# Opening of a two-layer trunk kernel: the modulation of chunks 6 and 7 computed by VectorE, and three scalings moved to ScalarE

## The chip, the cores and the metric

The kernel runs on one core of a Trainium2 chip. The metric is the device time of one execution in microseconds, the median of several runs. The engines of the core are TensorE (PE in the profile; its weight loads are PEld), VectorE (DVE), ScalarE (ACT) and GpSimd (POOL); SyncE (SP) issues most of the transfers from memory. Each engine works through a queue of its own in order, and engines wait for each other through semaphores.

## What is computed

The reference is a trunk of two layers over 512 tokens of width 1024 (a gated short convolution, then a state-space mixer, each followed by a SwiGLU network). Only its first steps matter here:

```python
mod = (jax.nn.silu(c) @ ada_w + ada_b).reshape(bsz, DEPTH, 2, 3, D_MODEL)
...
shift, scale, gate = (mod[:, i, 0, k][:, None, :] for k in range(3))
h = rmsnorm(x, norm_g[i, 0]) * (1.0 + scale) + shift
...
b_gate, c_gate, v = jnp.split(h @ w_in, 3, axis=-1)
u = causal_depthwise_conv(c_gate * v, conv_w)
return (b_gate * u) @ w_out
```

So a vector c of 1024 values is multiplied with columns of a wide matrix `ada_w` to give shift and scale, h is scaled and shifted with them, and h is multiplied with `w_in`. All of it is float32. A float32 product of the large kind is made of three products of rounded parts (high x high, high x low, low x high).

## The kernel before: how the opening is built

Channels lie in partitions: the 1024 channels are eight chunks (j = 0 to 7) of 128 partitions, and h_j is a tile of 128 x 512 (tokens) with a high and a low part. The opening builds h_0 to h_7 one by one, and uses each at once: six blocks of columns of `w_in` (128 columns each: two of c_gate, two of v, two of b_gate) are accumulated in six PSUM banks over the eight chunks, so that TensorE has work as soon as h_0 exists.

The order of all engines' instructions in this part is written out by hand in the table `OPENING`. Each name is a step, and each engine's queue holds its instructions in the order of the table. The names that matter:

- A*j*, E*j*, T*j*, R*j* (`ada_first`): shift and scale of chunk j. A: TensorE multiplies c with the 2 x 128 columns of `ada_w` for this chunk (16 products whose moving operand is the matrix; four strips of the array at once). E: ScalarE copies the result to `ada_acc`. T: TensorE transposes it, two products. R: VectorE sums the four strips, adds the bias, and makes the factor `acol`.
- u*j*, H*j*, l*j* (`make_h`): u is scale and shift by VectorE, H the same by ScalarE with rounding (the high part), l the difference of the two by VectorE (the low part).
- wcl*k*, wsl*k*, wcb*k*, wsb*k*: the weights of chunks k and k + 1 (from k = 2 on), rounded by ScalarE (c) and their low parts by VectorE (s); l is for column blocks 0 to 3, b for 4 and 5.
- k*j*_*i*: three matmuls of 512 columns, chunk j into column block i (high x high; high weight x low h; low weight x high h). k*j*_4 and k*j*_5 use the b weights.

The columns of `ada_w` come by SP's queue in the order of the code: `stage_cols(3, 2)` loads chunks 3 and 4 together, 256 columns (1 KB of each row), and at wsb1 `stage_cols(5, 2)` does so for 5 and 6, in four transfers of 512 KB. At A4 the weights of chunks 6 and 7 (three transfers) and `stage_cols(7, 1)` follow, which reads 128 columns (512 B of each row) in two transfers of 512 KB. At k2_5 ScalarE issues two small loads of its own, `rows` (the convolution's taps) and `dtb`.

Each transfer takes one of eight semaphores (DMAHW0 to DMAHW7) in turn; before it is issued it waits until the transfer before it on this semaphore has landed. The turns are given out in the order in which the compiler places the transfers, with those of SP and ScalarE mixed.

Behind the opening stands the loop of line 1047 and following over the remaining columns of `w_in`. Its first instructions on ScalarE are the copy c_sb of column block 0 (`gate_c(0)`), the rounding of the first weights (`split(0)`), and c_sb of block 1; on VectorE the low part of those weights (also `split(0)`) and cv = block 2 x c_sb (`gate_v(0)`). TensorE's first matmul of this loop (tile ip) uses the PSUM bank of block 2, which cv frees.

Of the kernel before, what the change touches and what calls it, by code (L numbers as in the profile page):

```python
# [8 lines left out]
F32 = mybir.dt.float32  # L9
# [7 lines left out]
P = 128  # L17
# [21 lines left out]
def trunk_kernel(  # L39
# [84 lines left out]
    def ada_madd(acc, w, k):  # L124
        if k == 0:
            dve.tensor_scalar(acc, w, csil[:, 0:1], None, MUL)
        else:
            dve.scalar_tensor_tensor(acc, w, csil[:, k:k + 1], acc, MUL, ADD)  # L128
# [223 lines left out]
    def make_h(s, j, hj, src, sl):  # L352

        n = sl.stop - sl.start
        q = s * 24 + j
        us = []

        def value():
            us.append(t2("u")[:, :n])
            dve.tensor_scalar(us[0], src, acol[:, s * 8 + j:s * 8 + j + 1], mods[:, q:q + 1], MUL, ADD)  # L360

        return (value, lambda: act.activation(hj[:, 0, sl], src, AF.Identity, bias=mods[:, q:q + 1],
                                       scale=acol[:, s * 8 + j:s * 8 + j + 1]),
                lambda: dve.tensor_tensor(hj[:, 1, sl], us[0], hj[:, 0, sl].bitcast(F32), SUB))
# [5 lines left out]
xo0 xo1 xo2 xo3 A0b xo4 E0 xo6 xo5 T0 wcl0 R0 u0 q7 H0 wsl0 wcb0 k0a0 l0 xo7 k0a1 k0a2 k0a3 wsb0  # L370
k0c0 k0_4 A1 k0_5 E1 wcl1 T1 k0c1 wcb1 R1 k0c2 k0c3 k0b0 u1 k0b1 H1 k0b2 wsl1 k0b3 l1 A2 wsb1 k1_0
E2 T2 k1_1 R2 wcl2 k1_2 u2 H2 k1_3 wsl2 k1_4 wcb2 l2 k1_5 wsb2 k2_0 k2_1 k2_2 A3 A4 E3 T3 E4 k2_3 R3
T4 u3 H3 k2_4 R4 k2_5 wcl4 l3 u4 H4 k3_0 wsl4 k3_1 wcb4 k3_2 l4 k3_3 wsb4 k3_4 k3_5 k4_0 A5 A6 E5 T5
E6 k4_1 R5 wcl6 T6 u5 k4_2 H5 R6 k4_3 u6 H6 k4_4 l5 wcb6 A7 l6 wsl6 k4_5 E7 T7 wsb6 k5_0 R7 k5_1 u7
k5_2 H7 k5_3 l7 k5_4 k5_5 k6_0 k6_1 k6_2 k6_3 k6_4 k6_5 k7_0 k7_1 k7_2 k7_3 k7_4 k7_5
"""


# [412 lines left out]
    with ExitStack() as ph:  # L791
# [79 lines left out]
        def stage_cols(j0, n):  # L871
            cols = ada_stage(j0, n, lambda: actp.tile([P, 8 // n, n * P], F32, tag="a", name="ada_st0"))
            staged.extend([(q, cols) for q in range(n)])

        xf = [xf2s[j // 2][:, j % 2, :] for j in range(KD)]
        xtr = []

# [24 lines left out]
        with tc.manual_schedule(engines={PE_ENGINE, mybir.EngineType.SP, mybir.EngineType.Activation,  # L902
# [68 lines left out]
            def kmm(kk, i, parts):  # L971
                k = kk % 2
                w, c0 = (lead[kk // 2][0], i * P) if i < 4 else (lead[kk // 2][1], (i - 4) * P)
                for part in parts:
                    pe.matmul(acc_of(i), w[:, part // 2, k, c0:c0 + P], h[kk][:, part % 2, :],  # L975
                              start=(kk, part) == (0, 0), stop=(kk, part) == (KD - 1, 2))

            def step(name):
                kind, i = name[:1], name[1:]
                if name[:2] == "xo":  # L980
                    turned_out(int(name[2:]))
                elif name == "q7":
                    xtr.append(aux_ps("xtr"))
                    for t in range(4):
                        turn(t, 7)
                    busy(acc_of(2)[:, :P], 5)
                    h.extend([hp.tile([P, 2, T], F32R, tag=f"h{j}", name=f"h{j}") for j in range(4, KD)])
                elif kind == "A":
                    j = int(i[0])
                    if j:  # L990
                        mods_[j] = ada_first(j, *staged[j], cpad)
                    next(mods_[j])
                    if j == 0:
                        busy(acc_of(2)[:, :P], 2)
                    if j == 4:
                        list(lead_load(3))
                        stage_cols(7, 1)
                elif kind in "ETR":
                    next(mods_[int(i)])
                elif kind in "uHl":  # L1000
                    j = int(i)
                    if j not in hdo:
                        hdo[j] = make_h(0, j, h[j], xf[j], FULL)
                    hdo[j]["uHl".index(kind)]()
                elif kind == "w":
                    kk = int(name[3:])
                    if kk // 2 not in lead:
                        lead_tiles(kk // 2)
                    lead_split(kk // 2, slice(kk % 2, kk % 2 + 1) if kk < 2 else slice(0, 2),
                               "lb".index(name[2]), "cs".index(name[1]))  # L1010
                    if name == "wsb1":
                        list(lead_load(2))
                        stage_cols(5, 2)
                elif name[:2] == "k0" and name[2] in "abc":
                    kmm(0, int(name[3]), ("abc".index(name[2]),))
                else:
                    kk, i = (int(q) for q in i.split("_"))
                    kmm(kk, i, (0, 1, 2))
                    if (kk, i) == (2, 5):
                        dma_s(rows[:24, 3, :], a_conv_w.rearrange("i k (r p) -> (i k r) p", p=P))  # L1020
                        dma_s(dtb[:NH], m_dt_bias.rearrange("i (r p) -> (i r) p", p=1))
                    if (kk, i) == (4, 5):
                        turned(rows[:24, 3, :], acw, 24)
# [1898 lines left out]
```

## Time and profile before

| | us |
|---|---|
| median of 3 runs | 1309.39 |
| lowest, highest run | 1309.07, 1309.95 |
| profiled execution, span from first to last instruction | 1307.2 |
| TensorE busy in the span | 1295.7 |
| opening: first ip matmul | 60.64 |

The profile has no other time of the profiled execution than its span. It is 2.2 us below the runs' median: starting and ending the program lie outside the span.

Rows of the timeline read: start in us, length in us, engine, line, operation, output<-inputs, shapes, and how many records the row merges; behind it, in brackets, how long the engine idled before and what ended that. A float32 product that isn't split into parts appears as two records. Rows of a table by stretches read: the stretch, its length, busy time of each engine with its records in brackets, the granted clock of TensorE, the share of the transfer engines and GB/s. Rows of groups end with busy us, mean ns of one, and idle time before.

### The profile page before, as it was taken

The numbers are of one execution on the slowest core, as the hardware profiler recorded it, in microseconds if no ns is written. First come the engines' busy times: TensorE is split into PE (matmuls) and PEld (weight loads), VectorE is DVE, ScalarE is ACT, GpSimd is POOL, SyncE is SP. The second block draws the span as 40 slices with busy tenths as digits, with TensorE's granted clock in tenths as the row PEclk, the third lists the DMA queues.
The fourth block names the chain that finished last, engine by engine and source line by source line (L and its number), as shares of the span: only waits on it lengthen the run. The fifth ranks groups of instructions, "written<-read, shape, count | busy, mean of one in ns | idle before, by whom it ended". The sixth has DMA issues, their size and how long they took to land.

```text
span 1307.2 us, 20568 instructions
## 1 busy us (share of the span) xinstructions
PE 1295.7 (99%) x7841; PEld 1140.6 (87%) x7841; DVE 1045.4 (80%) x1598; ACT 736.0 (56%) x1302; POOL 127.5 (10%) x156
## 2 busy tenths in 40 slices
PE   8999999999999999999999999999999999999998
PEld 7788889999988888898888888888899999998886
DVE  5587998978866986769899998987877777767888
ACT  5423466455532565656765567755764555544665
POOL 0000011111100230000000000000100121101320
PEclk9999999999999999999999999999999999999999
DMA  9779661799868984437664456614432788878961
GB/s 310 229 257 297 185 193 50 204 239 240 202 190 264 261 158 119 144 118 231 219 216 160 141 177 217 185 50 161 145 98 72 190 221 204 205 194 286 176 123 64
DMA packets 225942, 241.69 MB, mean 185 GB/s; under 512 B 10532, under 2 KB 177588, under 8 KB 224820
## 3 DMA queue, kind: packets, MB, share of 16 engines
q1 hardware_dynamic: 203200, 192.87, 47.3%
q0 software_dynamic: 18496, 35.92, 15.1%
q10 hardware_dynamic: 4148, 11.59, 2.7%
q8 instruction: 61, 1.00, 0.3%
q14 instruction: 37, 0.30, 0.1%
HBM read 203.76 MB, written 4.34 MB: 159 GB/s over the span
## 4 chain that ended last, share of the span: by engine, by line
PE 94%; DMA 2%; SPq 2%; DVE 1%; ACT 1%; issue 0%; DVEq 0%
PE sA L693 12%; PE ip L305 11%; PE ip L307 11%; PE ip L306 11%; PE y L408 7%; PE sC L693 6%; PE cA L2624 5%; PE sB L693 3%; PE cA L1483 3%; PE li L305 2%; PE li L307 2%; PE li L306 2%; PE li L975 2%; PE y L1156 1%; PE y L2199 1%; PE yd L2027 1%
## 5 line engine op out<-in xcount | busy, mean ns | idle before, releaser
L305 PE MATMUL ip<-h,whl 128*128 128x512 f32 x640 | 253.0, 395 | 0.2 <-DVE cv L1075 0.2
L307 PE MATMUL ip<-h,whl 128*128 128x512 f32 x640 | 249.7, 390 | 0.0
L306 PE MATMUL ip<-h,whl 128*128 128x512 f32 x640 | 249.6, 390 | 0.0
L305 PEld LDWEIGHTS ip<-h,whl 128*128 128x128 f32 x640 | 120.3, 188 | 25.8 <-issue 1.8
L307 PEld LDWEIGHTS ip<-h,whl 128*128 128x128 f32 x640 | 120.3, 188 | 25.3
L306 PEld LDWEIGHTS ip<-h,whl 128*128 128x128 f32 x640 | 120.4, 188 | 23.8
L693 PE MATMUL sA<-tq,whl 128*128 128x256 f32 x1008 | 130.6, 284 | 0.0
L693 PEld LDWEIGHTS sA<-tq,whl 128*128 128x128 f32 x1008 | 125.5, 192 | 0.3
L232 DVE TENSOR_TENSOR whl<-wst,whl 128x1024 fp32r<-128x1024 f32 x70 | 85.2, 1220 | 23.4 <-ACT whl L231 22.3
L128 DVE SCALAR_TENSOR_TENSOR ada_acc<-ada_st,csil,ada_acc 128x1024 f32<-128x1024 f32 x70 | 89.7, 1282 | 3.2 <-DMA ada_st<-in_ada_w_dram 1.9
L305 PE MATMUL li<-h,whl 128*128 128x256 f32 x288 | 83.7, 290 | 0.0
L307 PE MATMUL li<-h,whl 128*128 128x256 f32 x288 | 81.7, 284 | 0.0
L306 PE MATMUL li<-h,whl 128*128 128x256 f32 x288 | 81.6, 283 | 0.0
L231 ACT CAST whl<-wst 128x1024 fp32r<-128x1024 f32 x70 | 72.6, 1040 | 7.8 <-DMA wst<-in_a_w_in_dram 4.0
L408 PE MATMUL y<-whlo,ys 128*128 128x512 f32 x288 | 67.3, 392 | 0.0
L1870 DVE SCALAR_TENSOR_TENSOR cu<-ip,cols,cu 128x511 f32<-128x511 f32 (+2 forms) x84 | 62.8, 747 | 3.4 <-ACT cu L1867 1.4
L408 PEld LDWEIGHTS y<-whlo,ys 128*128 128x128 f32 x288 | 53.8, 188 | 11.4 <-issue 0.5
L2624 PE MATMUL cA<-whlo,ao 128*128 128x512 f32 x264 | 61.0, 391 | 0.4 <-DVE c L2830 0.2
L2624 PEld LDWEIGHTS cA<-whlo,ao 128*128 128x128 f32 x264 | 49.4, 188 | 11.5 <-ACT whlo L2589 1.2
L305 PEld LDWEIGHTS li<-h,whl 128*128 128x128 f32 x288 | 55.3, 192 | 0.8 <-issue 0.8
L306 PEld LDWEIGHTS li<-h,whl 128*128 128x128 f32 x288 | 55.3, 192 | 0.0
L307 PEld LDWEIGHTS li<-h,whl 128*128 128x128 f32 x288 | 55.2, 192 | 0.0
(457 smaller groups left out, 2740.8 us busy)
## 6 DMA issues: line engine op xcount, KB each, us to landing
ada_st<-in_ada_w_dram SPq DMA_DIRECT2D x96, 512.0 KB, 6.4
wsu<-in_f_w_in_dram SPq DMA_DIRECT2D x30, 512.0 KB, 5.5
sg<-in_f_w_in_dram SPq DMA_DIRECT2D x56, 256.0 KB, 3.4
wsu<-in_f_w_in_dram SPq DMA_DIRECT2D x56, 256.0 KB, 4.7
wst<-in_m_w_in_dram SPq DMA_DIRECT2D x14, 1024.0 KB, 5.9
wst<-in_f_w_in_dram SPq DMA_DIRECT2D x10, 1024.0 KB, 5.1
wst<-in_m_w_in_dram SPq DMA_DIRECT2D x20, 512.0 KB, 5.2
wst<-in_a_w_in_dram SPq DMA_DIRECT2D x9, 1024.0 KB, 6.8
```

The costliest lines, as they stand in the source:

```text
L128: dve.scalar_tensor_tensor(acc, w, csil[:, k:k + 1], acc, MUL, ADD)
L231: later.append((lambda sw=sw, w=w: act.copy(w[:, 0, :nk, :], sw), lambda sw=sw, w=w: dve.tensor_tensor(w[:, 1, :nk, :], sw, w[:, 0, :nk, : ...
L232: lambda sw=sw, w=w: dve.tensor_tensor(w[:, 1, :nk, :], sw, w[:, 0, :nk, :].bitcast(F32), SUB)))
L305: pe.matmul(dst, w_at(w, 0, kk), a[:, 0, sl], start=start, stop=False)
L306: pe.matmul(dst, w_at(w, 0, kk), a[:, 1, sl], start=False, stop=False)
L307: pe.matmul(dst, w_at(w, 1, kk), a[:, 0, sl], start=False, stop=stop)
L408: pe.matmul(pst, a[:, al, tk], wt[:, wl, kk, :], start=i == 0 and k == (opens[hf][t] if opens else 0), stop=k == K - 1 and i == 2, skip_gr ...
L693: pe.matmul(dst, w[:, wl, k0 + k, :], self.moving(q, k, al), skip_group_check=True, start=q in self.FIRST and k == 0 and i == 0, stop=k == ...
L975: pe.matmul(acc_of(i), w[:, part // 2, k, c0:c0 + P], h[kk][:, part % 2, :], start=(kk, part) == (0, 0), stop=(kk, part) == (KD - 1, 2))
L1483: pe.matmul(bank[r, sub], a[:, al, q, tk], w[:, wl, q, :], start=first and k == 0, stop=False, skip_group_check=True)
L1870: dve.scalar_tensor_tensor(u[:, sft:], pst[:, :T - sft], w[3 - sft], u[:, sft:], MUL, ADD)
L2624: pe.matmul(bank[r][sub], a[:, al, q, tk], w[:, hl, q, :], start=first and k == 0, stop=last and k == 2, skip_group_check=True)
```

## The change

Chunks 6 and 7 no longer use `ada_first`. Their columns of `ada_w` are loaded by the new `stage_one`, shift and scale columns side by side, in four transfers of 256 KB for each chunk. Chunk 5 is loaded alone. VectorE multiplies with c's values and adds up, row block by row block (steps M*j*_0 to M*j*_7, `one_madd`, 128 x 256 each); TensorE sums over the partitions by two products with a column of ones (P*j*, `one_sums`); VectorE adds the bias and makes the factor (G*j*, `one_mods`). For chunks 5, 6 and 7 u is made by ScalarE. The last chunk's matmuls are put in another order: first and third part of all six blocks (k7d0 to k7d5), then the second parts (k7b0 to k7b5).

```diff
         def value():
             us.append(t2("u")[:, :n])
-            dve.tensor_scalar(us[0], src, acol[:, s * 8 + j:s * 8 + j + 1], mods[:, q:q + 1], MUL, ADD)
+            if j < 5:
+                dve.tensor_scalar(us[0], src, acol[:, s * 8 + j:s * 8 + j + 1], mods[:, q:q + 1], MUL, ADD)
+            else:
+                act.activation(us[0], src, AF.Identity, bias=mods[:, q:q + 1], scale=acol[:, s * 8 + j:s * 8 + j + 1])
...
-T4 u3 H3 k2_4 R4 k2_5 wcl4 l3 u4 H4 k3_0 wsl4 k3_1 wcb4 k3_2 l4 k3_3 wsb4 k3_4 k3_5 k4_0 A5 A6 E5 T5
-E6 k4_1 R5 wcl6 T6 u5 k4_2 H5 R6 k4_3 u6 H6 k4_4 l5 wcb6 A7 l6 wsl6 k4_5 E7 T7 wsb6 k5_0 R7 k5_1 u7
-k5_2 H7 k5_3 l7 k5_4 k5_5 k6_0 k6_1 k6_2 k6_3 k6_4 k6_5 k7_0 k7_1 k7_2 k7_3 k7_4 k7_5
+T4 u3 H3 k2_4 R4 k2_5 wcl4 l3 u4 H4 k3_0 wsl4 k3_1 wcb4 k3_2 l4 k3_3 wsb4 k3_4 k3_5 M6_0 M6_1 M6_2 M6_3
+k4_0 A5 E5 T5 k4_1 R5 u5 H5 M6_4 M6_5 M6_6 M6_7 k4_2 l5 k4_3 wcl6 k4_4 P6 G6 u6 H6 wsl6 wcb6 l6 k4_5 wsb6
+M7_0 M7_1 M7_2 M7_3 M7_4 M7_5 M7_6 M7_7 k5_0 k5_1 k5_2 k5_3 k5_4 k5_5 k6_0 k6_1 k6_2 P7 G7 H7 u7 l7 k6_3
+k6_4 k6_5 k7d0 k7d1 k7d2 k7d3 k7d4 k7d5 k7b0 k7b1 k7b2 k7b3 k7b4 k7b5
...
+        def stage_one(j):
+            one_st[j] = [actp.tile([P, 4, 2, P], F32, tag="a", name="ada_st1") for _ in range(2)]
+            for q, st in enumerate(one_st[j]):
+                for b in range(2):
+                    dma(st[:, :, b, :], ada_w[q * T:(q + 1) * T, b * D + j * P:b * D + (j + 1) * P]
+                        .rearrange("(k p) f -> p k f", p=P))
+        def one_acc(j):
+            return ada_acc[:, 512 + (j - 6) * 256:768 + (j - 6) * 256]
+        def one_madd(j, k):
+            ada_madd(one_acc(j), one_st[j][k // 4][:, k % 4].rearrange("p b f -> p (b f)"), k)
+        def one_sums(j):
+            pt = one_sum[j] = aux_ps("ada_p1")
+            for b in range(2):
+                pe.matmul(pt[:, b:b + 1], one_acc(j)[:, b * P:(b + 1) * P], ones[:, 0:1], start=True, stop=True)
+        def one_mods(j):
+            m2, b2 = [v[:, 0:16].rearrange("p (a b) -> p a b", b=8)[:, :, j] for v in (mods, adab)]
+            dve.tensor_add(m2, one_sum[j][:, 0:2], b2)
+            dve.scalar_tensor_tensor(acol[:, j:j + 1], mods[:, 8 + j:9 + j], 1.0, ncol(0, 0, j), ADD, MUL)
...
-                              start=(kk, part) == (0, 0), stop=(kk, part) == (KD - 1, 2))
+                              start=(kk, part) == (0, 0), stop=(kk, part) == (KD - 1, 1))
...
-                        stage_cols(7, 1)
+                        stage_one(7)
...
-                        stage_cols(5, 2)
+                        stage_cols(5, 1)
+                        stage_one(6)
```

The first place is ScalarE's queue around step k2_5, and what its two small loads wait for. Before, from H3 (h_125) to wcb4 (whl_b):

```order
L362 ACTIVATE h_125<-xf,mods,acol 128x512 [waits DVE_49]
L1020 DMA rows<-in_a_conv_w_dram 24x128 [waits DMAHW3_49]
L1021 DMA dtb<-in_m_dt_bias_dram 32x1 [waits DMAHW5_49,Pool_49]
L845 CAST whl_l<-wst_l 128x1024 [waits DMAHW2_49]
L362 ACTIVATE h_305<-xf,mods,acol 128x512 [waits DVE_49]
L845 CAST whl_b<-wst_l 128x512 [waits DMAHW4_49]
```

The same place with the change:

```order
L365 ACTIVATE h_125<-xf,mods,acol 128x512 [waits DVE_49]
L1055 DMA rows<-in_a_conv_w_dram 24x128 [waits DMAHW5_49]
L1056 DMA dtb<-in_m_dt_bias_dram 32x1 [waits DMAHW7_49,Pool_49]
L849 CAST whl_l<-wst_l 128x1024 [waits DMAHW3_49,DMAHW2_49]
L365 ACTIVATE h_305<-xf,mods,acol 128x512 [waits DVE_49]
L849 CAST whl_b<-wst_l 128x512 [waits DMAHW4_49]
```

The instructions stand as they did, but the two loads have moved two semaphores on: rows from DMAHW3 to DMAHW5, dtb from DMAHW5 to DMAHW7.

The second place is SP's queue, where one sees which transfer was the last on these semaphores. A transfer that waits for DMAHW5 is itself the next one on DMAHW5. Before, chunks 5 and 6 (ada_st, 4 x 256) and the next weights (wst_l):

```order
L177 DMA ada_st_391<-in_ada_w_dram 128x4x256 [waits DMAHW5_49]
L177 DMA ada_st_393<-in_ada_w_dram 128x4x256 [waits DMAHW6_49]
L177 DMA ada_st_395<-in_ada_w_dram 128x4x256 [waits DMAHW7_49]
L177 DMA ada_st_397<-in_ada_w_dram 128x4x256 [waits DMAHW0_49]
L830 DMA wst_l<-in_a_w_in_dram 128x2x256 [waits DMAHW1_49,DVE_49]
L830 DMA wst_l<-in_a_w_in_dram 128x2x256 [waits DMAHW2_49]
L830 DMA wst_l<-in_a_w_in_dram 128x2x256 [waits DMAHW4_49]
```

With the change, chunk 5 (8 x 128), chunk 6 (4 x 128) and the same weights:

```order
L177 DMA ada_st_391<-in_ada_w_dram 128x8x128 [waits DMAHW5_49]
L177 DMA ada_st_393<-in_ada_w_dram 128x8x128 [waits DMAHW6_49]
L886 DMA ada_st_395<-in_ada_w_dram 128x4x128 [waits DMAHW7_49]
L886 DMA ada_st_395<-in_ada_w_dram 128x4x128 [waits DMAHW0_49]
L886 DMA ada_st_396<-in_ada_w_dram 128x4x128 [waits DMAHW1_49]
L886 DMA ada_st_396<-in_ada_w_dram 128x4x128 [waits DMAHW2_49]
L834 DMA wst_l<-in_a_w_in_dram 128x2x256 [waits DMAHW3_49,DVE_49]
```

Before, DMAHW5 was last taken by the first transfer of chunks 5 and 6. Now DMAHW5 is the first transfer of chunk 5, and DMAHW7 the first piece of chunk 6.

The third place is the end of TensorE's opening: chunk 7 (h_308) and the next loop's first matmul. Before, and now:

```order
L975 MATMUL li<-h_308,whl_l 128x512 x12
L975 MATMUL li<-h_308,whl_b 128x512 x6
L305 MATMUL ip<-h_122,whl 128x512
L306 MATMUL ip<-h_122,whl 128x512
L307 MATMUL ip<-h_122,whl 128x512
```

```order
L1005 MATMUL li<-h_308,whl_l 128x512 x8
L1005 MATMUL li<-h_308,whl_b 128x512 x4
L1005 MATMUL li<-h_308,whl_l 128x512 x4
L1005 MATMUL li<-h_308,whl_b 128x512 x2
L305 MATMUL ip<-h_122,whl 128x512
```

The same 18 matmuls of chunk 7: before, three at a time for each block; now two for each block, and then the third of each. ScalarE's and VectorE's instructions behind the opening (c_sb, the cast, c_sb; the split, cv) stand in the same order as before.

More of the change, by code (lines that the diff above doesn't have):

```diff
@@ L873, in stage_cols @@
             staged.extend([(q, cols) for q in range(n)])
+        one_st, one_sum = {}, {}
+        def stage_one(j):
[16 more added lines that the diff above has]
+            dve.scalar_tensor_tensor(acol[:, j:j + 1], mods[:, 8 + j:9 + j], 1.0, ncol(0, 0, j), ADD, MUL)
         xf = [xf2s[j // 2][:, j % 2, :] for j in range(KD)]
@@ L996, in step @@
                         list(lead_load(3))
-                        stage_cols(7, 1)
+                        stage_one(7)
+                elif kind == "M":
+                    one_madd(int(i[0]), int(i[2]))
+                elif kind in "PG":
+                    (one_sums, one_mods)["PG".index(kind)](int(i))
                 elif kind in "ETR":
@@ L1012, in step @@
                         list(lead_load(2))
-                        stage_cols(5, 2)
-                elif name[:2] == "k0" and name[2] in "abc":
-                    kmm(0, int(name[3]), ("abc".index(name[2]),))
+                        stage_cols(5, 1)
+                        stage_one(6)
+                elif name[2] in "abcd":
+                    kmm(int(name[1]), int(name[3]), {"a": (0,), "b": (1,), "c": (2,), "d": (0, 2)}[name[2]])
                 else:
```

## The prediction, made before the changed kernel had run

> **What bounds the kernel now.** I read the page's busy shares first, then the list of waits of TensorE, then the timeline of the opening.
>
> ```profile
> span 1307.2 us, 20568 instructions
> PE 1295.7 (99%) x7841; PEld 1140.6 (87%) x7841; DVE 1045.4 (80%) x1598; ACT 736.0 (56%) x1302; POOL 127.5 (10%) x156
> PE ip L305 <- DVE cv L1075: 0.2, 1, 0.2
> ```
>
> TensorE (PE) is busy for 99% of the span, and its queue is served in order. So a microsecond taken out of its queue, or a wait added to it, moves everything behind by as much: later stages have almost no idle time that could absorb it. The third row is the one wait where the opening hands over to the next loop; it becomes important below. The change touches only the stretch from 33 to 61 us, so I work there and carry the shift to the end unchanged.
>
> ```profile
> 39.67 0.84 PE L975 MATMUL li<-h,whl_l 128*128 128x512 f32 x3
> 40.44 1.95 PE L195 MATMUL ada_pe<-ada_st,rows 128*32 128x128 f32 x64
> 42.33 0.44 PE L202 MATMUL ada_pe<-ident,ada_acc 128*128 128x128 f32 x2
> 42.52 0.93 PE L975 MATMUL li<-h,whl_l 128*128 128x512 f32 x3
> 43.29 0.38 PE L202 MATMUL ada_pe<-ident,ada_acc 128*128 128x128 f32 x2
> 43.42 1.64 PE L975 MATMUL li<-h,whl_l 128*128 128x512 f32 x6
> ...
> 45.69 1.08 PE L195 MATMUL ada_pe<-ada_st,rows 128*32 128x128 f32 x32
> 46.70 0.97 PE L975 MATMUL li<-h,whl_b 128*128 128x512 f32 x3
> ...
> 47.76 0.44 PE L202 MATMUL ada_pe<-ident,ada_acc 128*128 128x128 f32 x2
> 47.95 0.47 PE L975 MATMUL li<-h,whl_l 128*128 128x512 f32 x1
> ```
>
> Matmuls overlap, so a cost on the path is the distance from one start to the next, not the length in the second column. k4_0 starts at 39.67, A5 and A6 take 40.44 to 42.33, T5 0.19, T6 0.13, A7 1.01 (45.69 to 46.70), T7 0.19.
>
> **Term 1, TensorE's work removed: -1.50 us.** T6, A7 and T7 go: 0.13 + 1.01 + 0.19 = 1.33. A6 goes too, but it had hidden E5. Now T5 stands straight behind A5 and waits for ScalarE's copy between them:
>
> ```profile
> 14.45 0.37 ACT L199 COPY ada_acc<-ada_pe 128x256 f32<-128x256 f32 x1
> 14.97 0.38 PE L202 MATMUL ada_pe<-ident,ada_acc 128*128 128x128 f32 x2
> 41.64 0.37 ACT L199 COPY ada_acc<-ada_pe 128x256 f32<-128x256 f32 x1 [3.72 <-PE ada_pe L195]
> ```
>
> E5 started 1.20 after A5 (41.64 against 40.44), lasts 0.37, and a transpose followed such a copy 0.15 after its end (14.82 to 14.97). So T5 stands 1.20 + 0.37 + 0.15 = 1.72 behind A5's start, where it was 1.89: of A6's 0.9 us only 0.17 is gained, the rest turns into a wait.
>
> **Term 2, the one-column products P6 and P7: +0.70 us.** No row shows a product with one moving column. Nearest by what sets it, a float32 product with full 128-column weights and few moving columns:
>
> ```profile
> 104.28 0.30 PE L148 MATMUL ada_ps<-fold,four 128*128 128x32 f32 x2
> 104.42 0.48 PE L305 MATMUL ip<-h,whl 128*128 128x512 f32 x1
> 2.48 4.64 PE L890 MATMUL xtr<-ident 128*128 128x128 f32 x20
> 15.62 1.28 PE L890 MATMUL li<-ident 128*128 128x128 f32 x10
> 11.48 0.64 PE L195 MATMUL ada_pe<-ada_st,rows 128*32 128x128 f32 x16 [1.06 <-DMA ada_st<-in_ada_w_dram]
> ```
>
> One product (two records) of 32 columns took 0.14 to the next start; each P has two: 0.28. From above, four records of 128 columns at 0.128 each (1.28/10) are 0.51. I take 0.35 for each P, near the fold's row. Nothing hides it, and nothing in these rows allows less than nothing.
>
> VectorE (DVE) must be ready for them. A multiply-add of this width:
>
> ```profile
> L720 DVE SCALAR_TENSOR_TENSOR g<-sA,g 128x256 f32<-128x256 f32 x14 | 5.9, 419 | 0.0
> ```
>
> Eight dependent ones are 8 x 0.42 = 3.4 us, with small gaps 3.6. M6's second half ends about 3.0 us after T5, while TensorE reaches P6 after 3.2 (T5 and four steps of about 0.75). From P6 to P7 TensorE has about 7.1 us (k4_5, the small transpose, k5, half of k6), and VectorE's queue (G6, the splits, the wait for H6, eight madds) needs about 7.0. Both just fit; I count 0, and up to +0.6 for the upper bound. The scalings that move to ScalarE (0.8 us each, as H4 at 36.60 below) have cover: u5 runs beside M6's second half, the wait for u6 is inside the 7.0, and u7 stands behind H7 and has the twelve matmuls k7d before l7 is needed.
>
> **Term 3, a wait on ScalarE's queue: +1.64 us.** Each transfer takes the next of eight semaphores, and waits until the transfer before it on that semaphore has landed. The two small loads that ScalarE issues at k2_5 thus wait for others. The order rows show that the second one (dtb) waited for the first 512 KB of chunks 5 and 6, on DMAHW5. Now six transfers stand there instead of four, and dtb comes to DMAHW7: the first 256 KB piece of chunk 6, that is 1.31 MB into this stretch of the queue, not 0.52. ScalarE is blocked meanwhile, with wcl4 and H4 behind it.
>
> ```profile
> 35.28 0.33 ACTq L1021 DMA_DIRECT2D dtb<-in_m_dt_bias_dram  x1
> 35.65 1.05 ACT L845 CAST whl_l<-wst_l 128x1024 fp32r<-128x1024 f32 x1 [0.92 <-DMA ada_st<-in_ada_w_dram]
> 36.60 0.81 ACT L362 ACTIVATE h<-xf,mods,acol 128x512 fp32r<-128x512 f32 x1
> 36.73 1.23 DVE L847 TENSOR_TENSOR whl_l<-wst_l,whl_l 128x1024 fp32r<-128x1024 f32 x1 [0.65 <-ACT whl_l L845]
> 37.87 0.68 DVE L364 TENSOR_TENSOR h<-u,h 128x512 fp32r<-128x512 f32 x1
> 24.00:29.00 5.00, 5.00 (x23) 4.09 (x24) 3.46 (x8) 2.65 (x4) 0.00 (x0) 1.00 1.10 349
> 41.00:43.00 2.00, 2.00 (x56) 1.76 (x49) 0.13 (x1) 0.86 (x3) 0.00 (x0) 1.00 1.19 293
> ```
>
> The cast's wait of 0.92 "<-DMA ada_st" is this one. The queue moved 349 GB/s where rows are 1 KB (24 to 29 us, chunks 3 and 4) and 293 where they are 512 B (41 to 43, chunk 7); chunks 5 and 6 are now read in 512 B rows. The first 512 KB had landed at 35.28, so the stretch began at 35.28 - 0.52/0.349 = 33.78. Now 1.31 MB at 293 GB/s end at 38.25: 2.97 later. Behind it l4 (37.87 to 38.55) ends at 41.52. k4_0's second matmul needs l4; it started about a third into k4_0, at 39.93. So TensorE stands until 41.57: 1.64 late, after a slack of 1.33 is used up. At 349 GB/s it would be 37.54, and 0.93 late: the lower bound.
>
> [...]
>
> **Term 4, the hand-over: +2.35 us.**
>
> ```profile
> 56.22 2.88 PE L975 MATMUL li<-h,whl_l 128*128 128x512 f32 x12
> 57.10 0.59 ACT L1071 COPY c_sb<-li 128x512 f32<-128x512 f32 x1 [7.13 <-PE li L975]
> 57.59 1.05 ACT L231 CAST whl<-wst 128x1024 fp32r<-128x1024 f32 x1
> 58.67 1.23 DVE L232 TENSOR_TENSOR whl<-wst,whl 128x1024 fp32r<-128x1024 f32 x1 [7.97 <-ACT whl L231]
> 59.81 0.68 DVE L1075 TENSOR_TENSOR cv<-li,c_sb 128x512 f32<-128x512 f32 x1
> 60.64 0.47 PE L305 MATMUL ip<-h,whl 128*128 128x512 f32 x1 [0.18 <-DVE cv L1075]
> ```
>
> The next loop's first matmul (ip) needs the bank that cv frees; cv stands behind c_sb, a cast and a split: from c_sb's start to ip 60.64 - 57.10 = 3.54 us, in order. c_sb starts when column block 0 is complete. Before, that was k7_0, the first 3 of the last 18 matmuls. These take (60.46 - 56.22)/18 = 0.236 each (60.46: ip less its wait); c_sb started 0.17 after the third. Now block 0 is complete only with k7b0, number 13 of 18, as the change does all first and third parts ahead: c_sb starts 5 x 0.236 - 0.17 = 1.01 before the queue's end, and ip 3.54 - 1.01 = 2.53 after it, where 0.18 was waited. TensorE stands still for 2.35 us more; the other matmuls are the same, so nothing pays for it.
>
> **Sum.** -1.50 + 0.70 + 1.64 + 2.35 = +3.19 us. The span of the profile would be 1310.4; what lies around it, 2.2 us between 1307.2 and the runs' median of 1309.39, stays: **1312.6 us**, 0.24% slower. What a measurement can tell from no change is about 0.2%, here 2.6 us, so a time above 1312.0 is "slower".
>
> **Rivals.**
>
> *Not slower: ScalarE isn't held up.* Place: the dtb load in ScalarE's queue. If the piece it waits for has landed by 35.28 + 1.33 = 36.6, not 38.25, term 3 is 0, and the sum -1.50 + 0.70 + 2.35 = +1.55: 1310.9. For it: the estimate goes by a mean rate. Against it: 1.6 us is half a megabyte at either rate.
>
> *Full rate.* Transfers of 512 B rows at 349: term 3 is 0.93, the sum +2.48, 1311.9. Against it: the row of 41 to 43 us. [...]
>
> *The saving wins.* If neither wait binds, terms 1 and 2 remain: -0.80, 1308.6. It would need ip's bank to come free without the chain of 3.54 us, which the wait of 0.18 in the trace speaks against. Faster by 2.6 is nearly excluded, as all of A6, T6, A7 and T7 are 2.3.
>
> *The array slows after the long wait.* In the row at 2.48 us, 20 records took 0.232 each, those at 15.62 us 0.128: TensorE starts at about half speed for some 4.6 us. If the 2.5 us of standing at the hand-over brought this back, as much would come on top as there, 4.64 - 20 x 0.128 = 2.1 us: 1314.7. It decides from some length of standing that the trace doesn't show: before the products at 11.48 us it stood 1.06 and did not slow down. [...]
>
> **Chances.** Forecast 0.62, with its own range from 1311.7 (349 GB/s and P at 0.28 each) to 1313.5 (P at 0.51, VectorE 0.6 late). Not held up 0.17, full rate 0.07, saving wins 0.08, array slows 0.06. The range 1310.8 to 1314.0 takes in the first three (0.86). Slower by over 0.2%: 0.53 of the forecast's 0.62 (its lowest part lies below 1312.0), 0.02 of full rate, the slowed array: 0.61. Faster by over 0.2%: 0.02. Within 0.2%: 0.37.
>
> **What would show it.** In the changed profile: dtb issued by ScalarE near 38.3 us, and TensorE waiting for H4 or l4 ahead of A5, 1.6 us in all; a wait of 0.7 us ahead of T5; P6 and P7 without long waits on the madds; and ip's wait on cv of about 2.5 us in place of 0.18. The prediction is wrong if dtb is issued before 36.6, or if cv no longer stands behind c_sb and the cast.

## The result and the profile after

| | before | after |
|---|---|---|
| median of 5 runs each, us | 1309.07 | 1318.23 |
| lowest, highest run | 1308.37, 1309.95 | 1316.40, 1318.94 |
| profiled execution, span | 1307.2 | 1317.2 |

The change makes the kernel slower: the ratio after to before is 1.0069, 95% interval 1.0057 to 1.0081. The forecast of 1312.6 had the sign, and with its +3.19 about a third of the 9.2 us; the time lies above its range. The page's row of busy times, then rows from TensorE's list of waits (total us, times, longest us), of the kernel after:

```profile
PE 1298.2 (99%) x7781; PEld 1140.6 (87%) x7781; DVE 1051.0 (80%) x1609; ACT 737.0 (56%) x1303; POOL 127.7 (10%) x156
```

```profile
PE ip L305 <- DVE cv L1110: 2.4, 1, 2.4
PE sA L697 <- ACT g L707: 1.9, 1, 1.9
...
PE li L1005 <- ACT h L365: 0.7, 1, 0.7
PE li L1005 <- DVE h L367: 0.7, 1, 0.7
PE ada_pe L202 <- ACT ada_acc L199: 0.5, 1, 0.5
```

Four of these five waits were forecast with their place and about their size. The wait of sA on g, 200 us behind the opening, was not. Where the time arises is seen by comparing the start of the same group of TensorE's matmuls in both traces (us; the shifts are taken from unrounded starts):

| group | before | after | shift | what lies between |
|---|---|---|---|---|
| A5 | 40.44 | 42.65 | +2.21 | waits for h4's two parts |
| T5 | 42.33 | 44.28 | +1.95 | |
| first ip | 60.64 | 64.77 | +4.13 | wait for cv |
| ada_ps | 104.28 | 109.95 | +5.66 | half clock behind the wait |
| sC | 251.67 | 257.51 | +5.84 | |
| sC, three groups later | 260.31 | 270.00 | +9.69 | wait of sA for g, and what follows it |
| last group | 1285.59 | 1295.39 | +9.80 | |

So three amounts: 4.13 in the opening (forecast 3.19), 1.53 right behind it, and 3.85 at 255 to 270 us. The two profiled executions differ by 10.0 us in their span, the medians by 9.2.

**The opening.** TensorE's timeline of the kernel after:

```profile
40.84 0.49 PE L1005 MATMUL li<-h,whl_l 128*128 128x512 f32 x1 [0.71 <-ACT h L365]
41.99 0.73 PE L1005 MATMUL li<-h,whl_l 128*128 128x512 f32 x2 [0.66 <-DVE h L367]
42.65 1.08 PE L195 MATMUL ada_pe<-ada_st,rows 128*32 128x128 f32 x32
44.28 0.44 PE L202 MATMUL ada_pe<-ident,ada_acc 128*128 128x128 f32 x2 [0.55 <-ACT ada_acc L199]
...
47.50 0.58 PE L898 MATMUL ada_p<-ones,ada_acc 128*128 128x1 f32 x4
47.94 0.94 PE L1005 MATMUL li<-h,whl_b 128*128 128x512 f32 x3
...
55.50 0.58 PE L898 MATMUL ada_p<-ones,ada_acc 128*128 128x1 f32 x4
...
64.77 0.77 PE L305 MATMUL ip<-h,whl 128*128 128x512 f32 x1 [2.44 <-DVE cv L1110]
65.34 0.63 PE L306 MATMUL ip<-h,whl 128*128 128x512 f32 x1
```

The one-column products take 47.94 - 47.50 = 0.44 for each P. The ip matmuls stand 0.43 us apart behind their wait, where the rows of the kernel before have 0.23. ScalarE and VectorE, same kernel:

```profile
38.60 0.33 ACTq L1056 DMA_DIRECT2D dtb<-in_m_dt_bias_dram  x1
39.02 1.05 ACT L849 CAST whl_l<-wst_l 128x1024 fp32r<-128x1024 f32 x1 [4.01 <-DMA rows<-in_a_conv_w_dram]
...
61.23 0.59 ACT L1106 COPY c_sb<-li 128x512 f32<-128x512 f32 x1 [3.21 <-PE li L1005]
61.72 1.05 ACT L231 CAST whl<-wst 128x1024 fp32r<-128x1024 f32 x1
```

```profile
45.30 2.05 DVE L128 SCALAR_TENSOR_TENSOR ada_acc<-ada_st,csil,ada_acc 128x256 f32<-128x256 f32 x4
...
51.74 3.61 DVE L128 SCALAR_TENSOR_TENSOR ada_acc<-ada_st,csil,ada_acc 128x256 f32<-128x256 f32 x7
...
62.80 1.23 DVE L232 TENSOR_TENSOR whl<-wst,whl 128x1024 fp32r<-128x1024 f32 x1 [4.05 <-ACT whl L231]
63.94 0.69 DVE L1110 TENSOR_TENSOR cv<-li,c_sb 128x512 f32<-128x512 f32 x1
```

dtb is issued at 38.60 (forecast 38.3) and holds the cast until 39.02. c_sb starts at 61.23, 3.54 ahead of ip: the chain of four keeps its length to the hundredth, and starts late because block 0 is complete late. The first two VectorE rows are the last multiply-adds of M6 and M7. They end at 47.35 and 55.35, and P6 and P7 start 0.15 us behind them (47.50 and 55.50): both products stood for VectorE, too briefly to appear in the list of waits.

**Right behind it, the clock.** The same kernel by stretches (length, busy time and records of PE, PEld, DVE, ACT, POOL, then the granted clock, the share of the transfer engines, GB/s). The bounds are those at which the granted clock changes in this trace:

```profile
61.21:64.62 3.41, 1.12 (x5) 0.58 (x4) 1.82 (x2) 2.02 (x3) 0.00 (x0) 1.00 0.00 0
64.62:68.03 3.41, 3.26 (x8) 2.61 (x9) 1.63 (x3) 1.66 (x2) 0.00 (x0) 0.50 0.00 0
...
259.18:262.59 3.41, 1.56 (x13) 1.36 (x13) 3.31 (x7) 2.61 (x6) 0.00 (x0) 1.00 0.73 175
262.59:266.01 3.42, 3.42 (x17) 3.42 (x18) 3.42 (x5) 1.04 (x2) 1.72 (x2) 0.50 1.06 290
```

Twice the clock is halved for 3.41 us, both times behind a stretch in which TensorE was busy for less than half (1.12 and 1.56 us).

**At 255 to 270 us.** VectorE's first write to the buffer raw1, before and after, and TensorE's wait that follows:

```profile
233.31 1.29 DVE L742 TENSOR_TENSOR raw<-h 128x512 f32<-128x512 f32 x2
```

```profile
243.03 1.29 DVE L746 TENSOR_TENSOR raw<-h 128x512 f32<-128x512 f32 x2 [3.97 <-PE li L307]
```

```profile
262.46 2.83 PE L697 MATMUL sA<-tq,whl 128*128 128x256 f32 x12 [1.85 <-ACT g L707]
```

The write that began at 233.31 before would begin near 239.0 with the 5.7 us of shift up to here; it begins at 243.03, as VectorE waited 3.97 us for a TensorE matmul. In the built program (its instructions with their waits, and the addresses of its tiles) this is a wait for memory: raw1 lies over two tiles of 4 KB per partition that held parts of the first weights of the SwiGLU network that follows (six blocks, two tiles each, used from 208 to 245 us in the kernel after), and before it may be written, the last matmul that reads them must be done. Before, that was a block used third; after, one used fifth. No line on raw1 was changed. The 22 slots of this pool are given out again in the order in which they came free; the first of chunk 6's staging tiles is now read by VectorE alone (M6_0 to M6_3) and comes free ahead of chunk 5's two, so the order in which slots 12, 3, 4 are given out again became 4, 12, 3, and all later tiles of the pool moved.

### The profile page after: what moved, and what is told of

Its sections match the earlier page's. It is cut to its first block, busy times and chain, and to the rows that moved or that the text cites. A ratio compares the mean times of both kernels' runs of the same rounds, so it can differ in the third digit from the quotient of the medians.

```text
span 1317.2 us, 20465 instructions
## 1 busy us (share of the span) xinstructions
PE 1298.2 (99%) x7781; PEld 1140.6 (87%) x7781; DVE 1051.0 (80%) x1609; ACT 737.0 (56%) x1303; POOL 127.7 (10%) x156
## 4 chain that ended last, share of the span: by engine, by line
PE 93%; SPq 2%; DVE 2%; DMA 2%; ACT 1%; issue 0%; DVEq 0%; ACTq 0%
PE sA L697 12%; PE ip L305 11%; PE ip L307 11%; PE ip L306 11%; PE y L412 7%; PE sC L697 6%; PE cA L2659 4%; PE sB L697 3%; PE cA L1518 3%; PE li L305 3%; PE li L307 3%; PE li L306 3%; PE y L1191 1%; PE y L2234 1%; PE li L1005 1%; PE yd L2062 1%
## 5 line engine op out<-in xcount | busy, mean ns | idle before, releaser
L128 DVE SCALAR_TENSOR_TENSOR ada_acc<-ada_st,csil,ada_acc 128x1024 f32<-128x1024 f32 (+1 forms) x84 | 96.5, 1149 | 3.7 <-DMA ada_st<-in_ada_w_dram 1.9
```

## The experiments

Theory from these rows: three separate causes, the hand-over (k7's order) with the half clock behind it, ScalarE's blocked queue, and the placement of raw1. Rival: the late wait is only a consequence of the delay. The kernel before was run again with each batch: 1308.69 (experiments 1 to 4), 1308.49 (5 to 8) and 1308.57 (9 to 11).

| no. | kernel | median us | ratio to before, 95% interval |
|---|---|---|---|
| 1 | after, raw1 elsewhere | 1312.61 | 1.0032 (1.0020 to 1.0044) |
| 2 | before, new order of k7 | 1311.95 | 1.0021 (1.0012 to 1.0031) |
| 3 | after, 8 products in the wait | 1316.37 | 1.0058 (1.0041 to 1.0074) |
| 4 | after, loads at the start | 1317.51 | 1.0067 (1.0052 to 1.0082) |
| 5 | after, 4 products in the wait | 1316.55 | one run |
| 6 | after, raw1 elsewhere, old hand-over | 1311.09 | 1.0016 (1.0007 to 1.0026) |
| 7 | 6, loads on SP | 1308.78 | 1.0001 (0.9992 to 1.0010) |
| 8 | 7, T5 behind k4_1 | 1309.07 | 1.0002 (0.9993 to 1.0010) |
| 9 | before, raw1 badly placed | 1313.61 | 1.0041 (1.0027 to 1.0054) |
| 10 | 8, two multiply-adds earlier | 1308.86 | 1.0001 (0.9992 to 1.0010) |
| 11 | after, 2 products in the wait | 1320.98 | one run |

**1. After, with raw1 in another place.** No instruction moves.

```diff
-        raw1 = sa.tile([P, 4, T], F32, tag="raw1", name="raw1")
-        raw3, raw2 = [sa.tile([P, 4, T], F32, tag=f"raw{q}", name=f"raw{q}") for q in (3, 2)]
+        raw3, raw1, raw2 = [sa.tile([P, 4, T], F32, tag=f"raw{q}", name=f"raw{q}") for q in (3, 1, 2)]
```

> The changed kernel with the tiles raw1 and raw3 laid down in the other order, so that raw1 no longer lies on the memory of the late lead weights; no instruction is moved. Theory (memory): VectorE's first write to raw1 waited 3.97 us for the last matmul on those weights, which made TensorE wait 1.9 us at sA and then run about 3.4 us at half the clock. So the wait of 3.97 and that at sA go, and with them 1.9 + about 1.5 us: near 1314.8. Rival (the chain is late because TensorE and the transfers of the opening moved against VectorE): the placing changes nothing, the wait at sA stays, 1318.2.

VectorE's row and the hand-over of this kernel, and its stretches on its own clock grid:

```profile
237.20 1.29 DVE L746 TENSOR_TENSOR raw<-h 128x512 f32<-128x512 f32 x2
```

```profile
64.55 0.47 PE L305 MATMUL ip<-h,whl 128*128 128x512 f32 x1 [2.44 <-DVE cv L1110]
64.85 0.39 PE L306 MATMUL ip<-h,whl 128*128 128x512 f32 x1
```

```profile
60.08:63.49 3.41, 2.02 (x9) 1.33 (x8) 0.92 (x1) 2.02 (x3) 0.00 (x0) 1.00 0.00 0
63.49:66.91 3.42, 2.36 (x10) 1.99 (x11) 1.63 (x3) 1.66 (x2) 0.00 (x0) 1.00 0.00 0
```

The wait of 3.97 and the one of sA are gone, and 5.6 us of time with them: more than expected. The reason is in the other rows: with the same wait of 2.44 the clock stayed full here, so this profile also lacks the 1.5 behind ip. What the clock does with a wait thus differs from run to run. That this median equals the forecast to the hundredth is luck: the opening holds ip up by 3.91 here, not 3.19, and the kernel before was 0.7 lower in this batch than when the forecast was made.

**2. Before, with nothing but the new order of chunk 7's matmuls** (k7d0 to k7d5, k7b0 to k7b5 in place of k7_0 to k7_5; `kmm` as in the change).

> The kernel before with one part of the change alone: chunk 7's matmuls in the new order (first and third parts of all blocks, then the second parts). Theory (hand-over and clock): ip waits on cv about 2.5 us instead of 0.18, and behind the wait the matmuls run at half the clock for some 3.4 us, which costs 1.5: 2.35 + 1.5 = 3.9, near 1313.0. Rival (the clock loss needs the other changes too, or comes from something else than the wait): the wait alone, 2.35, near 1311.4.

```profile
62.78 0.47 PE L305 MATMUL ip<-h,whl 128*128 128x512 f32 x1 [2.44 <-DVE cv L1075]
63.09 0.39 PE L306 MATMUL ip<-h,whl 128*128 128x512 f32 x1
...
63.63 0.63 PE L305 MATMUL ip<-h,whl 128*128 128x512 f32 x1
```

TensorE's rows. Without any other part of the change, ip waits 2.44 as in the kernel after and comes 62.78 - 60.64 = 2.14 late: term 4 (2.35) by itself. Two matmuls run at full pace behind the wait, and then the pace halves (0.63 for 0.39 in length): what halves it isn't tied to the wait's end. The runs spread from 1310.18 to 1313.05; their median of 1311.95 lies between the two expected times (1311.4 with a full clock, 1313.0 with the half stretch), so how often the clock is lost can't be told from it.

**3. After, eight products in the wait.**

```diff
             for name in OPENING.split():
                 step(name)
+            busy(one_sum[7][:, :P], 8)
```

> The changed kernel with eight unused 128 x 128 products (of the identity, into a bank that nobody reads any more) between the last matmul of the opening and the first ip matmul: about 2.05 us of work inside the wait of 2.44 us. Theory (clock): ip starts when it did, but the clock stays full: the first ip matmuls follow each other every 0.23 us instead of 0.43, 1.5 us are won, near 1316.7. Rival (the slow matmuls come from operands or other engines at the hand-over, not from the standing still): the pace stays 0.43 and the time 1318.2, or more by what the eight cost.

```profile
64.83 0.47 PE L305 MATMUL ip<-h,whl 128*128 128x512 f32 x1 [0.66 <-DVE cv L1110]
65.14 0.39 PE L306 MATMUL ip<-h,whl 128*128 128x512 f32 x1
```

ip starts when it did, but at full pace from the first matmul on: shift 4.33 at 251.67 instead of 5.84. So the 1.5 behind ip are the clock's, and TensorE's standing still is what takes them. The median is 1.9 lower than after (expected 1.5).

**4. After, the two small loads issued at the start** by ScalarE, so that they don't stand in its queue at k2_5.

```diff
             dma_s(rows[:96, 2, :], ada_b.rearrange("(r p) -> r p", p=P))
+            dma_s(rows[:24, 3, :], a_conv_w.rearrange("i k (r p) -> (i k r) p", p=P))
+            dma_s(dtb[:NH], m_dt_bias.rearrange("i (r p) -> (i r) p", p=1))
...
-                    if (kk, i) == (2, 5):
-                        dma_s(rows[:24, 3, :], a_conv_w.rearrange("i k (r p) -> (i k r) p", p=P))
-                        dma_s(dtb[:NH], m_dt_bias.rearrange("i (r p) -> (i r) p", p=1))
```

> The changed kernel with the two small loads that ScalarE issued at k2_5 (the convolution's taps and dtb) issued at the start, with the other small loads. Theory (ScalarE held up by the semaphore of dtb): the waits of 0.71 and 0.66 us ahead of and in k4_0 go, TensorE reaches the hand-over 1.4 us earlier; 1318.2 - 1.4 = 1316.8 if all behind it stays as it is. Rival (the weights of chunk 4 or its scale land late in any case): the waits stay, 1318.2.

```profile
40.49 1.08 PE L195 MATMUL ada_pe<-ada_st,rows 128*32 128x128 f32 x32
```

TensorE's A5 stands at 40.49 instead of 42.65 and both waits in k4_0 are gone: term 3 is the loads' wait. Of these 2.2 us the profiled execution still has 1.6 at its end (span 1315.6 for 1317.2), but the median is only 0.7 lower than after, within what the runs spread (1316.40 to 1318.94 in the kernel after). The new place has a price of its own at the start, where TensorE waited 1.7 us for xn (0.2 in the kernel after), but by 23.8 us this trace is level with that of after. Experiment 7 moves the loads elsewhere.

**5. After, four products in the wait**: as experiment 3, with 4.

> The changed kernel with four small products with the identity (into a bank that nothing reads) between the opening's last matmul and the next loop's first; they are extra, unused work. With eight of them the wait for cv shrank from 2.4 to 0.66 us and the granted clock stayed full, so four should leave about 1.5 us of wait. One single idle stretch of TensorE of 1.06 us kept the clock in the kernel before; 1.9 and 2.4 us lost it in the kernel after. If the length alone decides and the limit lies above 1.5 us: matmuls of the next loop 0.23 us apart from the first one, granted clock 1.00 in 60 to 75 us. If it lies below: 0.43 us apart for about 3.4 us, granted clock below 0.95 there. The second loss, near 262 us, should be seen again in both cases (a wait of 1.9 us and then half pace).

TensorE's rows, and the stretches on this trace's grid:

```profile
260.89 1.70 PE L697 MATMUL sA<-tq,whl 128*128 128x256 f32 x12 [1.85 <-ACT g L707]
...
266.88 1.69 PE L697 MATMUL sA<-tq,whl 128*128 128x256 f32 x12 [1.42 <-ACT g L707]
```

```profile
61.74:65.16 3.42, 1.87 (x13) 1.59 (x12) 1.82 (x2) 1.95 (x4) 0.00 (x0) 1.00 0.00 0
65.16:68.57 3.41, 3.41 (x17) 2.81 (x16) 2.17 (x3) 1.46 (x3) 0.00 (x0) 1.00 0.00 0
```

The wait of 1.55 kept the clock. The second part of the expectation missed: behind 1.85 us of waiting for g the clock stayed full as well, and TensorE waited a second time, 1.42. The sum is telling: between the same two sC groups this kernel loses 8.11 - 4.26 = 3.85, just as the kernel after does with its half clock (9.69 - 5.84). VectorE's lateness sets this amount; whether TensorE spends it at half clock or standing still made no difference.

**6. After, raw1 elsewhere and the old hand-over**: the edit of experiment 1, and

```diff
-k6_4 k6_5 k7d0 k7d1 k7d2 k7d3 k7d4 k7d5 k7b0 k7b1 k7b2 k7b3 k7b4 k7b5
+k6_4 k6_5 k7d0 k7b0 k7d1 k7b1 k7d2 k7b2 k7d3 k7b3 k7d4 k7b4 k7d5 k7b5
```

> The changed kernel with two edits: the buffers raw3 and raw1 are taken in the other order (raw1 then lies where an early-released tile lay), and the last 18 matmuls of the opening complete column block 0 after two steps (k7d0 k7b0 k7d1 k7b1 ...), as in the kernel before. Theory (placement and hand-over are each separate causes): the wait of 1.9 us near 260 us is gone, the wait for cv is 0.2 to 0.4 instead of 2.44, both stretches at half clock are gone. What is left of the +9.5 us: the two products P (0.88), the waits in k4_0 (1.37), the one ahead of T5 (0.55, in place of A6's work) less 2.3 of removed work, and up to 0.3 for l7 needed earlier: about 1309.5 to 1310.8 beside 1308.7 of the kernel before. Rival (the late wait comes with the delay of the opening itself and only moved in the run with the buffers exchanged): a wait of over 1 us remains near 250 to 262 us and the time stays above 1312.

The waits for cv and g are gone and the clock is full throughout; what is left is 2.6 us by the runs, 0.3 above the expected stretch. The rival is excluded.

**7. As 6, the small loads issued by SP** between the last lead block's loads and chunk 7's; ScalarE's two loads at k2_5 are taken out, as in experiment 4.

```diff
                         list(lead_load(3))
+                        dma(rows[:24, 3, :], a_conv_w.rearrange("i k (r p) -> (i k r) p", p=P))
+                        dma(dtb[:NH], m_dt_bias.rearrange("i (r p) -> (i r) p", p=1))
                         stage_one(7)
```

> As the run with exchanged buffers and the old hand-over, and the two small loads (convolution taps and dt bias) are issued by SP, between the fourth lead block's loads and chunk 7's, so that ScalarE's queue doesn't hold them. Theory: the waits of 0.71 and 0.66 us in k4_0 are gone, 1.2 to 1.4 us less than that run: about 1308.2 to 1309.6. Rival (the time lost in k4_0 is regained anyway, because later work waits for something else): same time as that run within 0.4 us.

```profile
60.84 0.47 PE L305 MATMUL ip<-h,whl 128*128 128x512 f32 x1
```

The time is 2.3 us less (expected 1.2 to 1.4): the two waits in k4_0 are 1.37 of idle time, but counted from start to start they held A5 up by 1.9 in the kernel after. ip is at 60.84 where the kernel before has 60.64. With three edits outside the new arithmetic the whole loss is gone. No gain is left that the runs can tell: the 2.3 us of work removed stand against the P's 0.88, T5's wait of 0.55, 0.43 by which TensorE stopped ahead of the two P (they start 0.39 and 0.50 behind the matmul ahead of them, not 0.23), and some 0.4 for chunk 7's low part, which is now needed two matmuls after its high part.

**8. As 7, T5 moved behind k4_1**, to give the copy E5 cover.

```diff
-k4_0 A5 E5 T5 k4_1 R5 ...
+k4_0 A5 E5 k4_1 T5 R5 ...
```

> As the run before (buffers, hand-over, loads on SP), and the transposes T5 stand behind k4_1 instead of straight behind A5, so that the copy E5 has cover. Theory: the wait of 0.55 us ahead of T5 is gone; TensorE then has 2.3 us of work less and 0.88 more than the kernel before and no new wait: 1307.3 to 1308.4, up to 0.1% faster than 1308.7. Rival (VectorE's multiply-adds of chunk 7 are late by what TensorE gains, as they end 4.1 us ahead of P7 at most): the wait moves to P7 or l7 and the time is that of the run before.

```profile
45.43 0.58 PE L898 MATMUL ada_p<-ones,ada_acc 128*128 128x1 f32 x4 [0.69 <-DVE ada_acc L128]
```

The wait ahead of T5 went and came back ahead of P6: the rival held in kind, though it named P7 or l7. VectorE's multiply-adds are the next bound.

**9. Before, raw1 placed over the sixth block.**

```diff
-        raw1 = sa.tile([P, 4, T], F32, tag="raw1", name="raw1")
-        raw3, raw2 = [sa.tile([P, 4, T], F32, tag=f"raw{q}", name=f"raw{q}") for q in (3, 2)]
+        raw2, raw3, raw1 = [sa.tile([P, 4, T], F32, tag=f"raw{q}", name=f"raw{q}") for q in (2, 3, 1)]
```

> The kernel before, with nothing but the order changed in which the three buffers raw1, raw2 and raw3 are taken, so that raw1 lies over a tile of the sixth lead block; its first write then waits for the last matmul of that block (before 239.3 us by the trace of the kernel before, where that write began at 233.3 us). Theory (placement alone makes the late wait, whatever the opening does): VectorE stands there for some 6 us, TensorE waits 3 to 4 us for g near 255 to 262 us, and loses one stretch at half clock as well (1.7): 1312 to 1314.5 beside 1308.5. Rival (the wait in the kernel after needs the late opening too): the write waits, but VectorE makes it up, no wait above 1 us on TensorE, 1308.5 within 0.8.

VectorE's row, and TensorE's stretches on this trace's grid:

```profile
238.92 1.30 DVE L742 TENSOR_TENSOR raw<-h 128x512 f32<-128x512 f32 x2 [4.70 <-PE li L307]
```

```profile
254.83:258.24 3.41, 1.68 (x14) 1.47 (x13) 3.31 (x6) 2.37 (x5) 0.00 (x0) 1.00 0.81 186
258.24:261.66 3.42, 3.31 (x27) 3.31 (x28) 3.42 (x6) 1.28 (x3) 1.62 (x2) 1.00 0.96 269
```

With the opening untouched, the exchange of three buffers costs 5.0 us, inside the expected stretch: placement is a cause by itself. The clock, expected to halve, stayed full: TensorE had been busy for 1.68 of the stretch's 3.41 us. As in experiment 5, the time was lost standing still.

**10. As 8, M6_4 and M6_5 ahead of R5 on VectorE.**

```diff
-k4_0 A5 E5 k4_1 T5 R5 u5 H5 M6_4 M6_5 M6_6 M6_7 ...
+k4_0 A5 E5 M6_4 M6_5 k4_1 T5 R5 u5 H5 M6_6 M6_7 ...
```

> As the run with T5 behind k4_1, and two of M6's last four multiply-adds (M6_4, M6_5) stand ahead of R5 on VectorE, in the 1.7 us in which it waited for T5. Theory: the wait of 0.69 us ahead of P6 goes, and M7 is early by as much, so P7 doesn't wait: 0.7 less than that run, 1308.0 to 1308.4, 0.0 to 0.1% faster than the kernel before. Rival (chunk 6's second half lands later than 41 us, or M7 just misses P7): a wait of 0.5 us or more on P6 or P7 and 1308.7 to 1309.1.

```profile
45.13 0.50 PE L898 MATMUL ada_p<-ones,ada_acc 128*128 128x1 f32 x4
45.49 0.93 PE L1005 MATMUL li<-h,whl_b 128*128 128x512 f32 x3
...
53.45 0.58 PE L898 MATMUL ada_p<-ones,ada_acc 128*128 128x1 f32 x4 [0.49 <-DVE ada_acc L128]
```

The wait moved on to P7: the rival held again. P6, which has its multiply-adds early here, takes 45.49 - 45.13 = 0.36 and stands 0.23 behind the matmul ahead of it; in the kernel after these are 0.44 each for the P, and 0.44 and 0.47 ahead of P6 and P7. No version beat the kernel before.

**11. After, two products in the wait**: as experiment 3, with 2, to see whether the clock keeps to fixed points 3.413 us apart in a new trace.

> The changed kernel with two small products with the identity (extra, unused work) between the opening and the next loop: about 2.0 us of wait for cv, and 1.85 us near 260 us. Theory of the grid: the granted clock changes only at fixed points 3.413 us apart, which the first change at the start of the trace gives (its phase differs from run to run); it halves for one such stretch if TensorE stood still for more than about half of the stretch before (1.55 us did not, 1.84 us did), and stays full if the wait is split so that neither part is above 1.55. So each of the two waits can be told from the start of this trace alone. Rival (the length of a wait decides): waits of 1.85 and 2.0 us both halve the clock, from the wait's end on.

The granted clock's first record in this trace is at 6.00 us; its first change to half, at 43.55, lies 11 x 3.413 behind that. On the grid from there:

```profile
40.13:43.55 3.42, 1.22 (x4) 0.48 (x4) 2.15 (x3) 2.27 (x3) 0.00 (x0) 1.00 0.92 278
43.55:46.96 3.41, 2.86 (x35) 1.64 (x35) 1.99 (x5) 0.37 (x1) 0.00 (x0) 0.50 1.15 309
46.96:50.37 3.41, 3.41 (x10) 2.73 (x10) 2.70 (x8) 2.28 (x3) 0.00 (x0) 0.50 0.93 301
...
64.03:67.44 3.41, 2.63 (x14) 2.08 (x12) 0.76 (x1) 2.02 (x3) 0.00 (x0) 1.00 0.00 0
67.44:70.85 3.41, 2.19 (x10) 1.87 (x11) 1.62 (x3) 1.67 (x2) 0.00 (x0) 1.00 0.00 0
262.00:265.41 3.41, 1.57 (x13) 1.36 (x13) 3.31 (x7) 3.13 (x6) 0.69 (x1) 1.00 0.79 221
265.41:268.83 3.42, 3.42 (x18) 3.42 (x18) 3.42 (x6) 0.53 (x1) 1.02 (x2) 0.50 1.13 280
```

All as the grid has it: the wait of 2.00 for cv is split by the bound at 67.44 and costs no clock; the 1.85 near 263 lie in one stretch and halve the next. In k4_0, where the loads landed later in this run (waits of 1.56 and 0.64), two waits in one stretch add up and halve the next. The clock did not come back behind that one, in which TensorE was busy for 2.86 of 3.41 us, but one stretch later. Why is open: at the start of experiment 4, where 16 records of products took 3.78 us, it came to full behind a stretch with 2.83 (4.32 to 7.73 us, on the grid back from 62.35). The rival, that a wait's length decides, is excluded: 2.00 did nothing here, 1.85 did.

## Why the prediction was wrong

**Right, with their sizes.** Term 1: T5 stands 1.63 behind A5 (forecast 1.72). Term 2: a P that need not wait takes 0.36 (P6 in experiment 10; forecast 0.35). Term 3: the mechanism held, and the queue moved 291 GB/s at 34 to 38.5 us (293 assumed); the two waits in k4_0 are 1.37 of idle time, and from start to start A5 is 2.21 late, of which 0.30 was there ahead of the first changed step, in the start of the program, which varies from run to run (TensorE's first wait is 2.3 us in the kernel before, 2.6 in the kernel after, 3.4 in experiment 2). That leaves 1.91 for the forecast's 1.64. Term 4: ip waits 2.44 (forecast 2.53), and experiment 2 has it alone.

**Too small: "I count 0" for VectorE's multiply-adds.** One of them takes 0.52 where 0.42 was read from a row, and P6 and P7 start 0.15 behind the last one, the distance that the prediction itself read between a copy and the transpose that needs it. Against the P6 of experiment 10, P6 lost 0.20 ahead of it, P7 0.24, and each 0.08 in it: 0.60 us in all, which is the upper bound that the prediction gave (0.6). Experiments 8 and 10 show that any gain ahead of the P meets VectorE. The sum of 3.19 came out as 4.13: 0.60 more from here, 0.27 from term 3 and the 0.30 of the start, less 0.09 each in terms 1 and 4; this closes within 0.1.

**Failed: "carry the shift to the end unchanged".** Its reason, that TensorE has almost no idle time later, excludes that the shift is absorbed, and says nothing on new waits. There was one: 3.85 us at 255 to 270 us, from where a buffer lies. The prediction read the change's edits on tiles (`ada_st1` in place of `ada_st`) as transfers only, and not as a change in who releases a slot of the shared pool and when. The built program showed it without a run: the first write to raw1 waits for a later matmul than before. Experiments 1 (taken away, with the change in place) and 9 (put in, without the change) show it from both sides.

**Failed: the chance of the slowed array, 0.06.** It was named at the right place, and with 2.1 against the 1.53 that came. Two things were wrong. The evidence against it, 1.06 us without a loss, was far from the 2.53 that were forecast. And it had a length of standing decide, which the runs don't bear out: in experiment 11 a wait of 2.00 us cost no clock and one of 1.85 did. What they show is fixed points 3.413 us apart: the two changes to half clock lie 58 of these steps from each other in the kernel after (64.62 and 262.59) and in experiment 4 (62.35 and 260.32), 65 in experiment 11 (43.55 and 265.41). And a stretch between two points need not be idle as a whole: with 1.57 us busy of 3.41 the clock was halved behind it (experiments 3 and 11), with 1.68 it was not (experiment 9). From these two I estimate that standing still for some 1.8 us of a stretch is the limit here, and that a wait of 2.44 halves the clock unless a bound leaves less than that on either side of it: 2 x 1.8 - 2.44 = 1.16 of 3.41 us, a third of the phases. Of the four traces with this wait (after, experiments 1, 2 and 4), three lost the clock. So the loss was the likely case, and the forecast should have had it in its sum: 1312.6 + 1.5 = 1314.1. That alone would not have reached 1318.2.

**What remains open.** TensorE's wait for ao near 450 us is 0.8 in the kernel after and between none and 0.9 in the other runs; it makes up to 0.9 of difference between two profiles, and no experiment was made on it. That the time after contains the half stretch behind ip rests on one profile. The four runs without a profile lie at 1316.4 to 1318.8, a spread that a loss of 1.5 in some and not in others would give; no second profile shows it.

## What to carry to other kernels

Where tiles come from a pool that hands out slots as they are released, giving a tile another reader can move every later tile of the pool; compare the waits of the whole built program, far from the edit too, before trusting that a shift is carried on unchanged. A work-saving edit on an engine that is 99% busy is worth what the waits it creates leave of it: here 2.3 us of matmuls were removed, and the new waits took back several times as much. Where TensorE stops for about as long as at this hand-over (2.44 us), count the half-speed stretch behind it (here 1.5 us) as part of its price, with a chance: here three of the four traces with this stop had it.

## What the runs showed of the hardware

- The granted clock changed at fixed points 3.413 us apart, whose phase differs from run to run (counted from the span's start 3.18 us in the kernel after, 2.00 in experiment 2, 0.91 in experiment 4). Up to the last matmuls it went to half after stretches with 0.97 to 1.57 us of TensorE busy (eight cases in five traces: the kernel after, experiments 2, 3, 4 and 11); in the stretches shown it stayed full after 1.68 (experiment 9) and more. Half clock lasted one stretch in seven of the cases; in the eighth it lasted two, and the first of these was busy for 2.86.
- The same wait of 2.44 us cost 1.5 us behind it in the kernel after and nothing in experiment 1. The kernel of experiment 2 ran in 1310.2 to 1313.1 with nothing changed; that the clock makes this spread fits, but is not shown, as only one of its runs has a profile.
- Half clock cost nothing where another engine was the bound: 3.85 us were lost between 255 and 270 us with it (the kernel after) and without it (experiment 5).
- Two float32 products with one moving column took 0.36 us to the next start (experiment 10), and 0.44 behind a stop (the kernel after); their four records stand 0.11 apart, hardly less than records of 128 columns (ten in 1.28).
- VectorE's dependent multiply-adds of 128 x 256 took 3.61 / 7 = 0.52 us each from start to start (forecast 0.42, with gaps 3.6 for eight; the eight of M7 took 3.99).
